# A bidirectional RWKV-7 layer on one core: readers of the side jobs' small products and the projections' evictions placed some dense blocks later, and their bank handed out in turn

## Chip, core and metric

The kernel runs on one core of a Trainium2 chip. The metric is the device time of one execution in microseconds; the number to forecast is the median over runs of the changed kernel. Before the change it is 3232.46 us (three runs, 3229.34 to 3234.77).

## What is computed

One layer over 128 context and 1024 latent tokens of width 1024: half a SwiGLU FFN, a token mixer, half a second FFN, each with a norm before and after and a modulation. The mixer is the part that the change touches. Cut to what matters:

```python
r, k, v, g, cb, cc, xc, gate_a, gate_b = split(h @ w_in)          # 5632 columns
kk = k*k_k;  kk = kk * rsqrt(sum(kk*kk over a head) + 1e-12)
for d in (0, 1):                                                   # forward, backward
    decay, a_d = small two-layer maps of h and its shifted copy
    k_d = k * (1 + (a_d - 1)*k_a)
    S = S*w_t + (S @ -kk_t) (kk_t*a_t)^T + v_t k_t^T ;  y_t = S @ r_t   # per head, per token
y = groupnorm(y_0 + y_1)*gn_gain + gn_bias + (bonus_0 + bonus_1)*v
y_a = (y*sigmoid(g)) @ w_branch_a
y_b = (cb * conv3(cc*xc)) @ w_branch_b
out = (sigmoid(gate_a)*y_a + sigmoid(gate_b)*y_b) @ w_out
```

## The kernel before

All tokens lie along the free axis in three tiles of 384; every dense product is float32 made of three fp32r matmuls (low weights by high input, high by low, high by high). Such a triple, 128 input rows deep, is called a *block* here. A projection column of `w_in` (128 outputs) takes 3 tiles by 8 blocks. The mixer has 1056 of them, numbered 1 to 1056 in the order in which TensorE runs them (L740 to L742, function `proj`).

The recurrence is done in chunks of 64 tokens, as 18 **items** (16 for the latent tokens, two heads' pairs `g` by eight steps `j`; 2 for the context). An item has three parts:

- `front` (function `stage_b`, once for each direction): loads of the operands, products `scr` (L1047) and `bkt` (L1062), masks, four copies `nn` (L1056);
- `solve`: the triangular systems, almost all of it on VectorE. It begins with one transpose `lm` (L1079), of which there is one for each item, goes through 15 pairs of a product `un` and a sum (L1088, L1089), a pair of transposes `xr` (L1108, L1109), and ends with small products `l64`, `l64b` on TensorE (L1116, L1127);
- `seq_latent` or `seq_ctx` (function `step`): two steps of the states in each direction (L1165 to L1199).

In step i the program writes front(i+1), the states of item i, solve(i+1). These three are called the **chain**, and get the highest priority with the scheduler, which puts the instructions of each engine into one fixed order. An engine runs its list in that order.

Beside the chain there are **side jobs**: `stage_k` (the normed kk and the bonus of one pair of heads and 256 tokens), `stage_v` (v turned into the state's layout), `finish` (group norm and gate of the result). Each is a generator that gives back, after each piece, a number of blocks to wait for. Three lanes (f, k, v) hold them. `fill(n)` takes n blocks from the projections (`filler`); after each it may advance one lane by one piece, and sets `PB.anchor` to that block. An instruction passed through `PB` is ordered behind the anchor on its engine's list. The small products of side jobs (`cps`, `kkb`, `bon`, `vt`, `gv`, `gm`, all at L177 by the wrapper) write to one PSUM bank, tag "oc", of which there is a single buffer. Their reader on VectorE or ScalarE follows in the program directly, with no anchor of its own (`rsq` at L238, L970, L978, L997, L1229).

The main loop has two ways of using up blocks: `fill(GI)` with GI = 40 after each item, and

```python
        def need(kind, g, *bs):
            while not all((kind, 2 * g + pp, b) in made for b in bs for pp in range(2)):
                fill(1)
```

before an item whose input a side job must have finished. Blocks used in `need` run beside side jobs only; the chain has nothing to do there once it has run dry. When `filler` is empty, `fill` goes on calling side jobs and gives TensorE nothing.

The projections' results are copied out of PSUM by ScalarE at `evict()`, called at the second block of the next tile (L750).

Of the kernel before, what the change touches and what calls it, by code (L numbers as in the profile page):

```python
# [13 lines left out]
AF = mybir.ActivationFunctionType  # L14
ALU = mybir.AluOpType
# [45 lines left out]
def body(ctx: ExitStack, tc: tile.TileContext, I: dict, y_prompt, y_sample, new_state):  # L61
# [120 lines left out]
    PB = Beside()  # L182
# [50 lines left out]
            V.scalar_tensor_tensor(out=y, in0=tt, scalar=1.5, in1=y, op0=ALU.add, op1=ALU.mult)  # L233
        return y

    def rsq(ps, n, scale, eps):
        x = tiny.tile([128, 16], F32, name="nx", tag="nx")[:, :n]
        V.tensor_scalar(out=x, in0=ps[:, :n], scalar1=scale, scalar2=eps, op0=ALU.mult, op1=ALU.add)  # L238
        return newton(x, n)

    def compact(sq, n, rhs, nr, scale, eps, tag="sc", PE=PE):
        ps = psp.tile([128, 16], F32, name="cps", tag=tag, bufs=1 if tag == "oc" else 2)
        for i in range(n):
            PE.matmul(ps[:, i * nr:(i + 1) * nr], sq[:, i * 128:(i + 1) * 128], rhs, start=True, stop=True)
        return rsq(ps, n * nr, scale, eps)

    def bcast(rs, sp, PE=PE):
        ps = psp.tile([128, TW], F32, name="bcps", tag="sc")
# [410 lines left out]
def mixer(nc, tc, pool, env):  # L659
# [68 lines left out]
    def proj(col, evac, ts=range(NT)):  # L728

        if col not in ahead:  # L730
            assert not plan or plan[0] == col
            if plan:
                fetch()
            else:
                ahead[col] = load_w(w_in[:, col:col + 128], 8, G)
        w = ahead.pop(col)
        for t in ts:
            ps = e.psp.tile([128, TW], F32, name="pj", tag="mm")
            for k, ((hi, lo), (xh, xl)) in enumerate(zip(w, hx(t))):
                PE.matmul(ps, lo, xh, start=(k == 0), stop=False)  # L740
                PE.matmul(ps, hi, xl, start=False, stop=False)  # L741
                ins = PE.matmul(ps, hi, xh, start=False, stop=(k == 7))  # L742
                clock["dense"] += 1
                if k == 0 and t == ts[0]:
                    fetch(ins)
                if k == 5 and t == ts[len(ts) > 1]:
                    for job in halves:
                        job()
                    halves.clear()
                if k == 1:  # L750
                    evict()
# [47 lines left out]
    with ExitStack() as ph:  # L799
# [15 lines left out]
            G.memset(t_, 0.0)  # L815
        HR = [slice(0, 64), slice(64, 128)]

        GI, GF, GL, GM, GC, SG_ = 40, 8, 16, 6, 14, 2
        def job_g(p):
            yield from proj(1536 + p * 128, to_dram(gd[p], AF.Tanh, scale=0.5))  # L820
            evict()
# [117 lines left out]
            return out  # L939


        def stage_k(p, t0, n, bon=True):

            while ("rkv", p) not in made:
                yield 1
            nt = n // 128
            k = q1.tile([128, 256], F32, name="ok", tag="ok")[:, :n]
            turned(k, mirrored(p, 5, -1, t0, n), PB.first)
            r = oload(opd[p][:, 3], t0, n, "or")
            f0, f1 = (q1.tile([128, 256], F32, name=f"o{x}", tag=f"o{x}")[:, :n] for x in "di")  # L950
            turned(f0, mirrored(p, 2, -1, t0, n))
            turned(f1, mirrored(p, 7, -1, t0, n))
            yield GL
            a = q1.tile([128, 256], F32, name="oa", tag="oa")[:, :n]
            PB.first(S.activation(out=a, in_=k, func=AF.Square, scale=e.KK_[:, p:p + 1]))
            b = f0
            PB.first(V.tensor_tensor(out=b, in0=f0, in1=f1, op=ALU.add))
            V.tensor_tensor(out=b, in0=b, in1=k, op=ALU.mult)
            V.scalar_tensor_tensor(out=b, in0=r, scalar=rk4[:, p:p + 1], in1=b, op0=ALU.mult, op1=ALU.mult)
            v = r  # L960
            SP.dma_start(v, vd[p][:, t0:t0 + n])
            yield 3
            rs = compact(a, nt, sel, 2, 1.0, 1e-12, "oc", PB)
            yield GC
            ps = ps_.tile([128, 256], F32, name="kkb", tag="oc", bufs=1)[:, :n]
            for i in range(nt):
                for h in range(2):
                    PB.matmul(ps[HR[h], i * 128:(i + 1) * 128], rs[:, 2 * i + h:2 * i + h + 1].to_broadcast([128, 64]), ident, start=True, stop=True)
            kk = a
            V.scalar_tensor_tensor(out=kk, in0=k, scalar=e.KK_[:, p:p + 1], in1=ps, op0=ALU.mult, op1=ALU.mult)  # L970
            for h, dst in enumerate(mirrored(p, 4, 1, t0, n)):
                SP.dma_start(dst, kk[HR[h]])
            made.add(("kk", p, (t0 - NCTX) // 256))
            yield 4
            ps = ps_.tile([128, 256], F32, name="bon", tag="oc", bufs=1)[:, :n]
            PB.matmul(ps, bones, b, start=True, stop=True)
            o = v
            V.tensor_tensor(out=o, in0=v, in1=ps, op=ALU.mult)  # L978
            S.activation(out=o, in_=o, func=AF.Identity, bias=gb4[:, p:p + 1])
            SP.dma_start(bvd[p][:, t0:t0 + n], o)  # L980
            yield GF

        def stage_v(p, t0, n, zv):
# [4 lines left out]
                yield 1  # L988
            v = oload(vd[p], t0, n, "lv", PB.first)
            yield GL  # L990
            ps = ps_.tile([128, 4, 64], F32, name="vt", tag="oc", bufs=1)
            for i in range(nb):
                for h in range(2):
                    hr, kr = HR[h], HR[1 - h]
                    PB.matmul(ps[kr, i], v[hr, i * 64:i * 64 + 64], cent[hr] if t0 >= NCTX else ident[hr, hr], start=True, stop=True)
            for h in range(2):
                S.activation(out=zv[HR[1 - h], 0:nb, p % 2, HR[h]], in_=ps[HR[1 - h], 0:nb], func=AF.Copy)  # L997
            made.add(("vt", p, (t0 - NCTX) // 256))

        def turned(dst, srcs, first=lambda ins: None):  # L1000
# [206 lines left out]
        def finish(p, t0, n, y):  # L1207
# [5 lines left out]
            yc = q1.tile([128, 256], F32, name="yc_", tag="f3")[:, :n]  # L1213
            yo = y
            if t0 < NCTX:
                ps = ps_.tile([128, 256], F32, name="gm", tag="oc", bufs=1)[:, :n]
                PB.matmul(ps, bones, y, start=True, stop=True)
                V.scalar_tensor_tensor(out=yc, in0=ps, scalar=-1.0 / 64, in1=y, op0=ALU.mult, op1=ALU.add)
                yo = yc
            a = q1.tile([128, 256], F32, name="ysq", tag="f4")[:, :n]  # L1220
            PB.first(S.activation(out=a, in_=yo, func=AF.Square))
            yield GM
            rs = compact(a, nt, sel, 2, 1.0 / 64, 64e-5, "oc", PB)
            yield GC
            ps = ps_.tile([128, 256], F32, name="gv", tag="oc", bufs=1)[:, :n]
            for i in range(nt):
                for h in range(2):
                    PB.matmul(ps[HR[h], i * 128:(i + 1) * 128], rs[:, 2 * i + h:2 * i + h + 1].to_broadcast([128, 64]), ident, start=True, stop=True)
            V.tensor_tensor(out=yc, in0=yo, in1=ps, op=ALU.mult)  # L1229
# [293 lines left out]
```

## Time and profile before

| | us |
|---|---|
| median of three runs | 3232.46 |
| lowest, highest | 3229.34, 3234.77 |
| the profiled execution's own time | 3226.22 |
| its span, first to last instruction | 3224.3 |

Busy shares over the span: TensorE 93%, VectorE 57%, ScalarE 36%, GpSimd 14%. They are means over stages that are limited by different things. The scan with its side jobs and projections takes the stretch from about 1060 to 2131 us; ahead of it lie the first FFN and the two-layer maps, behind it the two branches, the output projection and the second FFN.

To read it: of a stretch of the span, the windows view gives the busy time of each engine with the number of its instructions in parentheses, then the granted TensorE clock (1.00 is full speed), the share of the DMA engines and the bytes moved. Since the chain begins anew with each `lm`, the time between two `lm` is the length of an item.

### The profile page before, as it was taken

Reading aid. Unit: us, or ns where it says so; the run is one execution under the profiler, and the core shown is the slowest. Engines: PE = TensorE matmul, PEld = TensorE weight load, DVE = VectorE, ACT = ScalarE, POOL = GpSimd, SP = SyncE. Lnnn points to the kernel's source line nnn. Section 1 sums busy time; section 2 is a strip of 40 time slices with the busy share of each in tenths; the row PEclk is TensorE's granted clock in tenths of the full one; section 3 lists DMA queues with packets and bytes.
Section 4 is the critical chain, followed back from the end, with each engine's and each line's share of the span. In section 5 each row is a group of like instructions: output and inputs, shape, how many; then the busy total and the mean of one; then the engine's idle time right before and its main releaser. Section 6 shows DMA issues by size and latency. Waiting matters only on the chain.

```text
span 3224.3 us, 55042 instructions
## 1 busy us (share of the span) xinstructions
PE 3005.2 (93%) x21284; PEld 2836.3 (88%) x21284; DVE 1821.8 (57%) x4148; ACT 1151.7 (36%) x2618; POOL 453.8 (14%) x436
## 2 busy tenths in 40 slices
PE   8999999999989989988898898679989999999998
PEld 5999999999979987877777777469989999999998
DVE  7535655654875344566875668665782323323356
ACT  5421121113545424354544445332543111121244
POOL 1000000000241121333322322100220000000012
PEclk9999999999989999999999999779989999999999
DMA  8422333324534542322333223236432111111244
GB/s 271 148 63 85 111 89 92 99 79 126 163 118 133 178 132 66 111 81 79 90 114 105 88 86 108 62 112 190 141 99 66 46 38 49 46 38 45 84 144 131
DMA packets 483898, 330.80 MB, mean 103 GB/s; under 512 B 49768, under 2 KB 461748, under 8 KB 483636
## 3 DMA queue, kind: packets, MB, share of 16 engines
q1 hardware_dynamic: 483008, 326.80, 33.9%
q8 instruction: 167, 2.74, 0.4%
q14 instruction: 95, 0.78, 0.1%
q10 hardware_dynamic: 308, 0.44, 0.0%
q0 software_dynamic: 320, 0.04, 0.0%
HBM read 265.58 MB, written 61.60 MB: 101 GB/s over the span
## 4 chain that ended last, share of the span: by engine, by line
PE 69%; DVE 17%; ACT 5%; issue 4%; DMA 3%; POOL 1%; SPq 0%; DVEq 0%; ACTq 0%; POOLq 0%
PE po L220 6%; PE po L219 6%; PE po L221 6%; PE pg L220 5%; PE pg L219 5%; PE pg L221 5%; PE pu L220 5%; PE pu L219 5%; PE pu L221 5%; PE pj L742 3%; PE pj L740 3%; PE pj L741 3%; DVE un L1088 2%; PE scr L1047 2%; DMA ops<-opd 1%
## 5 line engine op out<-in xcount | busy, mean ns | idle before, releaser
L138 ACT ACTIVATE whi<-wst 128x512 fp32r<-128x512 f32 (+1 forms) x578 | 350.4, 611 | 731.6 <-PE po L221 393.1
L139 DVE TENSOR_TENSOR wlo<-wst,whi 128x512 fp32r<-128x512 f32 (+1 forms) x480 | 326.7, 681 | 305.4 <-ACT whi L138 296.1
L740 PE MATMUL pj<-hh,wlo 128*128 128x384 f32 x1056 | 375.4, 355 | 0.3 <-ACT fso L768 0.3
L741 PE MATMUL pj<-hl,whi 128*128 128x384 f32 x1056 | 371.1, 351 | 2.7 <-POOL hl L269 1.4
L742 PE MATMUL pj<-hh,whi 128*128 128x384 f32 x1056 | 371.3, 352 | 0.0
L220 PE MATMUL pg<-hl,whi 128*128 128x384 f32 x1056 | 356.8, 338 | 5.3 <-POOL hl L269 2.9
L219 PE MATMUL po<-ah,wlo 128*128 128x384 f32 x1056 | 357.1, 339 | 3.8 <-ACT ah L138 3.8
L219 PE MATMUL pg<-hh,wlo 128*128 128x384 f32 x1056 | 357.7, 339 | 1.9 <-DVE wlo L139 1.3
L220 PE MATMUL po<-al,whi 128*128 128x384 f32 x1056 | 356.3, 338 | 0.4 <-DVE al L139 0.4
L221 PE MATMUL pg<-hh,whi 128*128 128x384 f32 x1056 | 356.1, 337 | 0.0
L221 PE MATMUL po<-ah,whi 128*128 128x384 f32 x1056 | 355.7, 337 | 0.0
L219 PE MATMUL pu<-hh,wlo 128*128 128x384 f32 x1056 | 355.4, 337 | 0.0
L220 PE MATMUL pu<-hl,whi 128*128 128x384 f32 x1056 | 354.0, 335 | 0.0
L221 PE MATMUL pu<-hh,whi 128*128 128x384 f32 x1056 | 354.0, 335 | 0.0
L279 POOL TENSOR_TENSOR ss<-ss,sqt 128x384 f32<-128x384 f32 x78 | 88.7, 1140 | 1695.8 <-ACT sqt L278 1691.3
L432 DVE TENSOR_TENSOR sil<-sil,pu 128x384 f32<-128x384 f32 x132 | 72.8, 552 | 352.7 <-PE pu L221 352.6
L404 DVE TENSOR_TENSOR o<-o,po 128x384 f32<-128x384 f32 x288 | 159.0, 552 | 172.4 <-PE po L221 171.4
L741 PEld LDWEIGHTS pj<-hl,whi 128*128 128x128 f32 x1056 | 204.3, 193 | 9.9 <-issue 3.0
L740 PEld LDWEIGHTS pj<-hh,wlo 128*128 128x128 f32 x1056 | 203.7, 193 | 10.4 <-issue 5.7
L742 PEld LDWEIGHTS pj<-hh,whi 128*128 128x128 f32 x1056 | 204.2, 193 | 7.4 <-issue 3.3
L220 PEld LDWEIGHTS pg<-hl,whi 128*128 128x128 f32 x1056 | 200.1, 189 | 7.8 <-DVE hl L271 3.9
L219 PEld LDWEIGHTS po<-ah,wlo 128*128 128x128 f32 x1056 | 198.6, 188 | 4.8 <-ACT ah L138 4.8
(584 smaller groups left out, 5746.9 us busy)
## 6 DMA issues: line engine op xcount, KB each, us to landing
wst<-in_ffn_w SPq DMA_DIRECT2D x324, 256.0 KB, 2.9
wmod<-in_w_mod SPq DMA_DIRECT2D x144, 256.0 KB, 2.8
wst<-in_w_in SPq DMA_DIRECT2D x94, 256.0 KB, 3.3
ops<-opd SPq DMA_DIRECT2D x36, 640.0 KB, 4.5
wst<-in_ffn_w SPq DMA_DIRECT2D x96, 192.0 KB, 2.5
xo<-xd SPq DMA_DIRECT2D x64, 192.0 KB, 3.9
wst<-in_w_out SPq DMA_DIRECT2D x48, 256.0 KB, 2.8
opd<-zv SPq DMA_DIRECT2D x24, 384.0 KB, 2.8
```

Of the source, the lines that this page charges most:

```text
L138: first(S.activation(out=hi, in_=src, func=AF.Copy))
L139: eng.tensor_tensor(out=lo, in0=src, in1=hi.bitcast(F32), op=ALU.subtract)
L219: PE.matmul(ps, lo, xh, start=(k == 0), stop=False)
L220: PE.matmul(ps, hi, xl, start=False, stop=False)
L221: later.tick(PE.matmul(ps, hi, xh, start=False, stop=(k == nk - 1)))
L279: eng.tensor_tensor(out=ssum, in0=ssum, in1=q, op=ALU.add)
L404: V.tensor_tensor(out=O[m][t], in0=O[m][t], in1=ps, op=ALU.add)
L432: V.tensor_tensor(out=s, in0=s, in1=pu, op=ALU.mult)
L740: PE.matmul(ps, lo, xh, start=(k == 0), stop=False)
L741: PE.matmul(ps, hi, xl, start=False, stop=False)
L742: ins = PE.matmul(ps, hi, xh, start=False, stop=(k == 7))
L1047: PE.matmul(ps[64 * o:64 * o + 64, i], BK[64 * h:64 * h + 64, o, i * 64:i * 64 + 64], E[64 * h:64 * h + 64, s0 + i, h], start=True, stop=True)
```

## The change

1. `evict()` is called at the fourth block of the next tile and not at the second.
2. The reader of each small product is given back to the lane for GV = 4 blocks more, and is then ordered behind the block that is current (`PB.first`).
3. A lock: a job that wants the bank calls `take()`, which waits in steps of 7 blocks while another job holds it; after the reader the lock is cleared.

Arithmetic, operands and transfers stay the same.

```diff
-    def rsq(ps, n, scale, eps):
+    def rsq(ps, n, scale, eps, first=lambda ins: None):
...
-        V.tensor_scalar(out=x, in0=ps[:, :n], scalar1=scale, scalar2=eps, op0=ALU.mult, op1=ALU.add)
+        first(V.tensor_scalar(out=x, in0=ps[:, :n], scalar1=scale, scalar2=eps, op0=ALU.mult, op1=ALU.add))
...
-                if k == 1:
+                if k == 3:
                     evict()
...
-        GI, GF, GL, GM, GC, SG_ = 40, 8, 16, 6, 14, 2
+        GI, GF, GL, GM, GC, SG_, GV = 40, 8, 16, 6, 14, 2, 4
...
+        held = []
+
+        def take():
+
+            while held:
+                yield 7
+            held.append(1)
...
-            rs = compact(a, nt, sel, 2, 1.0, 1e-12, "oc", PB)
+            yield from take()
+            ps = e.sums(a, nt, sel, 2, "oc", PB)
+            yield GV
+            rs = e.rsq(ps, 2 * nt, 1.0, 1e-12, PB.first)
+            held.clear()
             yield GC
+            yield from take()
             ps = ps_.tile([128, 256], F32, name="kkb", tag="oc", bufs=1)[:, :n]
...
-            V.scalar_tensor_tensor(out=kk, in0=k, scalar=e.KK_[:, p:p + 1], in1=ps, op0=ALU.mult, op1=ALU.mult)
+            yield GV
+            PB.first(V.scalar_tensor_tensor(out=kk, in0=k, scalar=e.KK_[:, p:p + 1], in1=ps, op0=ALU.mult, op1=ALU.mult))
+            held.clear()
```

The same three lines (`take`, `yield GV`, `PB.first` with the lock cleared) go round `bon`, `vt`, both products of `finish`, and, without the wait, `gm`.

Both kernels have the same 1056 blocks, but they stand elsewhere against the chain. Line numbers of the changed kernel are 3 higher in `proj` and 24 higher from `stage_b` on.

**First place: TensorE, where item 2 begins.** `pj` is a block's matmul, `hhT_t` its input (row group, then tile of tokens), `scr` the first product of the item's `front`, `sq` and `yp` those of the states. Before:

```order
L740 MATMUL pj_12694<-hh7_0_8311,wlo_12569 128x384
L741 MATMUL pj_12694<-hl7_0_8312,whi_12568 128x384
L742 MATMUL pj_12694<-hh7_0_8311,whi_12568 128x384
L740 MATMUL pj_12745<-hh0_1_8826,wlo_12565 128x384
L741 MATMUL pj_12745<-hl0_1_8827,whi_12564 128x384
L742 MATMUL pj_12745<-hh0_1_8826,whi_12564 128x384
L1047 MATMUL scr_12922<-e0_12905,ops_12907 64x128
```

Now:

```order
L743 MATMUL pj_13156<-hh1_2_9343,wlo_12962 128x384
L744 MATMUL pj_13156<-hl1_2_9344,whi_12961 128x384
L745 MATMUL pj_13156<-hh1_2_9343,whi_12961 128x384
L743 MATMUL pj_13156<-hh2_2_9352,wlo_12962 128x384
L1071 MATMUL scr_13401<-e0_13384,ops_13386 64x128
```

The first `scr` of item 2 stood behind block 393; it stands behind block 498 now, four projection columns later.

**Second place: TensorE, where the blocks end.** `l64` is the product that ends a solve, `cps`, `gv`, `kkb` and `bon` are products of side jobs. Before:

```order
L740 MATMUL pj_21574<-hh7_2_9402,wlo_21047 128x384
L741 MATMUL pj_21574<-hl7_2_9403,whi_21046 128x384
L742 MATMUL pj_21574<-hh7_2_9402,whi_21046 128x384
L1186 MATMUL yp_21364<-ab0_20604,zv2_9436 64x64 x4
L1186 MATMUL yp_21364<-ab1_20605,zv1_9435 64x64 x4
L1177 MATMUL yp_21770<-e0_21187,zv0_9434 64x64 x4
L1177 MATMUL yp_21770<-e1_21188,zv0_9434 64x64 x4
L177 MATMUL cps_21522<-cst_81,ysq_21499 128x2 x2
```

Now:

```order
L743 MATMUL pj_18865<-hh7_2_9401,wlo_18658 128x384
L744 MATMUL pj_18865<-hl7_2_9402,whi_18657 128x384
L745 MATMUL pj_18865<-hh7_2_9401,whi_18657 128x384
L1071 MATMUL scr_18946<-e1_18878,ops_18931 64x128
L1071 MATMUL scr_18947<-e1_18878,ops_18931 64x128
```

The last block stood in the middle of item 16; it now stands ahead of the second `front` of item 10.

**Third place: TensorE, the end of the solve of item 11.** Before:

```order
L742 MATMUL pj_18733<-hh1_0_8144,whi_18295 128x384
L740 MATMUL pj_18733<-hh2_0_8173,wlo_18296 128x384
L741 MATMUL pj_18733<-hl2_0_8174,whi_18295 128x384
L1127 MATMUL l64b_18167<-xr_18138,x8_18104 32x32
L1165 MATMUL sq_18471<-zv3_9437,e1_17859 64x64 x4
L1165 MATMUL sq_18471<-zv0_9434,e0_17858 64x64 x4
L1127 MATMUL l64b_18168<-xr_18138,x8_18104 32x32
L1047 MATMUL scr_18380<-e0_18363,ops_18365 64x128 x8
```

Now:

```order
L1140 MATMUL l64_19525<-xr_19522,ab0_19237 32x32 x2
L1140 MATMUL l64_19525<-xr_19522,ab1_19238 32x32 x2
L1151 MATMUL l64b_19551<-xr_19522,x8_19488 32x32
L1189 MATMUL sq_19722<-zv3_9437,e1_19243 64x64 x4
L1189 MATMUL sq_19722<-zv0_9434,e0_19242 64x64 x4
L1151 MATMUL l64b_19552<-xr_19522,x8_19488 32x32
L1071 MATMUL scr_19631<-e0_19614,ops_19616 64x128 x8
```

The chain's products keep their own sequence; the blocks between them are gone, here and in every item from 11 on. Counted over the whole list, the blocks ahead of the first products of the two directions' fronts are:

| front of item | 0 | 1 | 2 | 9 | 10 | last block |
|---|---|---|---|---|---|---|
| before, 1st / 2nd direction | 214 / 259 | 295 / 296 | 393 / 438 | 717 / 718 | 758 / 809 | in item 16 |
| now | 260 / 316 | 353 / 354 | 498 / 554 | 829 / 831 | 1006 / 1056 | in item 10 |

## Rows read from the trace of the kernel before

**Rows 1.** The page: busy times by engine; TensorE's granted clock in 40 slices.

```profile
PE 3005.2 (93%) x21284; PEld 2836.3 (88%) x21284; DVE 1821.8 (57%) x4148; ACT 1151.7 (36%) x2618; POOL 453.8 (14%) x436
...
PEclk9999999999989999999999999779989999999999
```

**Rows 2.** Windows view of the mixer's stretches: PE, PEld, DVE, ACT, POOL, PEclk, DMA, GB/s.

```profile
1351.00:1664.00 313.00, 272.58 (x2987) 233.72 (x2986) 229.74 (x667) 143.38 (x394) 107.29 (x105) 0.95 0.32 92
1664.00:1724.00 60.00, 56.68 (x745) 44.80 (x736) 41.44 (x135) 32.71 (x98) 14.31 (x15) 1.00 0.31 91
1767.00:2030.00 263.00, 234.47 (x2666) 200.22 (x2662) 181.75 (x543) 128.52 (x368) 77.72 (x79) 0.96 0.33 97
2030.00:2069.00 39.00, 22.23 (x326) 18.45 (x328) 30.17 (x102) 14.57 (x40) 7.50 (x9) 0.78 0.25 76
2069.00:2131.00 62.00, 31.81 (x392) 24.11 (x392) 39.66 (x165) 14.46 (x50) 1.15 (x4) 0.56 0.09 24
```

**Rows 3.** Source view of the transpose that begins each solve; then VectorE's timeline at two.

```profile
L1079 DVE STREAM_TRANSPOSE lm<-nn x18: 1231/1239/1246, 1190.7 to 2069.3; 128x1024 f32<-128x1024 f32 x18
...
1767.49 1.25 DVE L1079 STREAM_TRANSPOSE lm<-nn 128x1024 f32<-128x1024 f32 x1
...
2030.23 1.24 DVE L1079 STREAM_TRANSPOSE lm<-nn 128x1024 f32<-128x1024 f32 x1
```

**Rows 4.** Timeline of TensorE at 2030 us: third matmul of consecutive blocks (start, us).

```profile
2030.91 0.33 PE L742 MATMUL pj<-hh,whi 128*128 128x384 f32 x1
...
2031.95 0.34 PE L742 MATMUL pj<-hh,whi 128*128 128x384 f32 x1
```

**Rows 5.** Windows view of 20 us inside a wait for side jobs.

```profile
1280.00:1300.00 20.00, 20.00 (x121) 19.52 (x120) 8.92 (x21) 5.37 (x11) 6.11 (x6) 1.00 0.17 47
```

**Rows 6.** Groups by line on VectorE, 1351 to 1664 us: busy us, mean ns, idle before.

```profile
L848 DVE SCALAR_TENSOR_TENSOR cnv<-ccs,cw,cnv 128x378 f32<-128x378 f32 (+2 forms) x12 | 9.2, 770 | 0.0
L232 DVE TENSOR_TENSOR nt<-nt,nx 128x4 f32<-128x4 f32 x36 | 8.3, 231 | 0.1
L233 DVE SCALAR_TENSOR_TENSOR ny<-nt,ny 128x4 f32<-128x4 f32 x36 | 7.4, 205 | 0.1
L847 DVE SCALAR_TENSOR_TENSOR cnv<-ccs,cw,cnv 128x378 f32<-128x378 f32 (+2 forms) x12 | 6.9, 575 | 2.0 <-ACT cnv L842 1.9
L231 DVE SCALAR_TENSOR_TENSOR nt<-ny 128x4 f32<-128x4 f32 x36 | 6.3, 174 | 0.1
L957 DVE TENSOR_TENSOR od<-od,oi 128x256 f32<-128x256 f32 x6 | 4.9, 822 | 0.0
L978 DVE TENSOR_TENSOR or<-or,bon 128x256 f32<-128x256 f32 x5 | 2.0, 402 | 2.8 <-PE bon L177 2.8
L238 DVE TENSOR_SCALAR nx<-cps 128x4 f32<-128x4 f32 x12 | 1.9, 154 | 3.2 <-PE cps L177 3.1
```

**Rows 7.** Waits, 1135 to 2140 us: total, times, longest.

```profile
ACT fso L768 <- PE pj L742: 77.7, 34, 4.5
DVE nx L238 <- PE cps L177: 41.0, 17, 8.3
DVE oa L970 <- PE kkb L177: 25.4, 7, 5.9
DVE or L978 <- PE bon L177: 17.3, 9, 2.9
```

**Rows 8.** Timeline: one form on VectorE beside GpSimd's weight split and without it.

```profile
1492.26 1.51 DVE L1040 TENSOR_TENSOR e<-ops,fl 64x256 f32<-64x256 f32 x1
...
1490.79 2.71 POOL L139 TENSOR_TENSOR wlo<-wst,whi 128x512 fp32r<-128x512 f32 x2 [2.79 <-ACT whi L138]
...
2036.55 0.41 DVE L1040 TENSOR_TENSOR e<-ops,fl 64x256 f32<-64x256 f32 x1
```

**Rows 9.** Timeline of TensorE: 16 products of a front at either clock.

```profile
1424.97 1.09 PE L1047 MATMUL scr<-e,ops 64*64 64x128 f32 x16
...
2057.73 1.97 PE L1047 MATMUL scr<-e,ops 64*64 64x128 f32 x16
```

More of the change, by code (lines that the diff above doesn't have):

```diff
@@ L234, in newton, with sums @@
         return y
-    def rsq(ps, n, scale, eps):
+    def rsq(ps, n, scale, eps, first=lambda ins: None):
         x = tiny.tile([128, 16], F32, name="nx", tag="nx")[:, :n]
-        V.tensor_scalar(out=x, in0=ps[:, :n], scalar1=scale, scalar2=eps, op0=ALU.mult, op1=ALU.add)
+        first(V.tensor_scalar(out=x, in0=ps[:, :n], scalar1=scale, scalar2=eps, op0=ALU.mult, op1=ALU.add))
         return newton(x, n)
-    def compact(sq, n, rhs, nr, scale, eps, tag="sc", PE=PE):
+    def sums(sq, n, rhs, nr, tag="sc", PE=PE):
         ps = psp.tile([128, 16], F32, name="cps", tag=tag, bufs=1 if tag == "oc" else 2)
@@ L244, in compact @@
             PE.matmul(ps[:, i * nr:(i + 1) * nr], sq[:, i * 128:(i + 1) * 128], rhs, start=True, stop=True)
-        return rsq(ps, n * nr, scale, eps)
+        return ps
+    def compact(sq, n, rhs, nr, scale, eps, tag="sc", PE=PE):
+        return rsq(sums(sq, n, rhs, nr, tag, PE), n * nr, scale, eps)
     def bcast(rs, sp, PE=PE):
@@ L974, in stage_k @@
             yield 4
+            yield from take()
             ps = ps_.tile([128, 256], F32, name="bon", tag="oc", bufs=1)[:, :n]
@@ L977, in stage_k @@
             o = v
-            V.tensor_tensor(out=o, in0=v, in1=ps, op=ALU.mult)
+            yield GV
+            PB.first(V.tensor_tensor(out=o, in0=v, in1=ps, op=ALU.mult))
+            held.clear()
             S.activation(out=o, in_=o, func=AF.Identity, bias=gb4[:, p:p + 1])
@@ L990, in stage_v @@
             yield GL
+            yield from take()
             ps = ps_.tile([128, 4, 64], F32, name="vt", tag="oc", bufs=1)
@@ L995, in stage_v @@
                     PB.matmul(ps[kr, i], v[hr, i * 64:i * 64 + 64], cent[hr] if t0 >= NCTX else ident[hr, hr], start=True, stop=True)
+            yield GV
             for h in range(2):
-                S.activation(out=zv[HR[1 - h], 0:nb, p % 2, HR[h]], in_=ps[HR[1 - h], 0:nb], func=AF.Copy)
+                PB.first(S.activation(out=zv[HR[1 - h], 0:nb, p % 2, HR[h]], in_=ps[HR[1 - h], 0:nb], func=AF.Copy))
+            held.clear()
             made.add(("vt", p, (t0 - NCTX) // 256))
@@ L1215, in finish @@
             if t0 < NCTX:
+                yield from take()
                 ps = ps_.tile([128, 256], F32, name="gm", tag="oc", bufs=1)[:, :n]
@@ L1219, in finish @@
                 yo = yc
+                held.clear()
             a = q1.tile([128, 256], F32, name="ysq", tag="f4")[:, :n]
@@ L1222, in finish @@
             yield GM
-            rs = compact(a, nt, sel, 2, 1.0 / 64, 64e-5, "oc", PB)
+            yield from take()
+            ps = e.sums(a, nt, sel, 2, "oc", PB)
+            yield GV
+            rs = e.rsq(ps, 2 * nt, 1.0 / 64, 64e-5, PB.first)
+            held.clear()
             yield GC
+            yield from take()
             ps = ps_.tile([128, 256], F32, name="gv", tag="oc", bufs=1)[:, :n]
@@ L1228, in finish @@
                     PB.matmul(ps[HR[h], i * 128:(i + 1) * 128], rs[:, 2 * i + h:2 * i + h + 1].to_broadcast([128, 64]), ident, start=True, stop=True)
-            V.tensor_tensor(out=yc, in0=yo, in1=ps, op=ALU.mult)
+            yield GV
+            PB.first(V.tensor_tensor(out=yc, in0=yo, in1=ps, op=ALU.mult))
+            held.clear()
             V.scalar_tensor_tensor(out=yc, in0=yc, scalar=gg4[:, p:p + 1], in1=bv, op0=ALU.mult, op1=ALU.add)
```

## Prediction

> **What bounds the kernel now.** I read the page first. TensorE is busy 93% of the span [rows 1], so at first sight only its work counts. The page's clock line falls in two places, and the second of them, ahead of the second FFN, is the end of the scan [rows 1]. So the next view is that of the windows over the scan. There TensorE is busy 272.58 of 313 us while items 2 to 8 run, and only 22.23 of 39 us in the item in which the blocks run out [rows 2]. VectorE is busy 229.74 of the same 313 us.
>
> Then the items themselves. There are 18 transposes that open a solve, the last at 2069.3 us; item 10's is at 1767.49, item 16's at 2030.23 [rows 3]. So six items with blocks among them take 262.7 us, 43.8 each. The seventh, which has only the last 7 blocks in its first microseconds, takes 39.0. This comparison decides the case. An item loses some 38 blocks and gets 5 us shorter, though a block alone takes TensorE 0.52 us (two of them from 2030.91 to 2031.95) [rows 4], and 38 take 20 us. An item is therefore not as long as TensorE's work but as long as the chain, which lies mostly on VectorE: 30.17 us busy in the item without blocks, 181.75/6 = 30.3 in those with them [rows 2]. The blocks fill TensorE's waiting time. A block put beside the chain is nearly free; one that runs where the chain stands still costs its whole 0.52 us. In such a stretch TensorE is full: 121 matmuls in 20.00 busy us of 20 [rows 5].
>
> **The change part by part.** It adds no matmul, no operation and no transfer; the lock is the generator's, and no engine sees it. What it moves is the place of the blocks, and this the order of the changed kernel shows exactly.
>
> *Blocks put ahead of the chain, first part.* Three lanes now wait in turn for one bank, in steps of 7 blocks, and each of their products holds it for 4 blocks more. The items' `need` goes on drawing blocks until the jobs are through. The second front of item 2 comes 554 blocks in, before it was 438. The side jobs ahead of it are the same, so the 116 blocks are bare: 116 x 0.52 = **+60 us**.
>
> *Items 2 to 8.* From that front to the first of item 9 there are 275 blocks for 279: **-2 us**.
>
> *Second part.* From item 9's first front to item 10's there were 41 blocks and are 177. 136 x 0.52 = 71 us. The old stretch took 60 us with 3.3 us of TensorE idle [rows 2]; I set that against the products of the side jobs that are run there now instead of in items 2 to 8. **+71 us**.
>
> *What items 2 to 8 lose.* Some side jobs and projections no longer meet the chain there, since they run in the two stretches above. Of the three convolutions' 216 blocks 118 remain, so 45% of 9.2 + 6.9 us on VectorE go: -7. Of 12 root computations 8 remain; their 23.9 us (1.9 + 6.3 + 8.3 + 7.4) are 2.0 each: -8. Two `stage_k` and three `finish` fewer have 19 other operations, at 402 ns as the bonus reader: -8. The waits for `cps` and `bon`, which later readers are spared, are 3.2 + 2.8: -6. All from [rows 6]; together -29 us. VectorE is busy 73% of that stretch, and what leaves in its idle time gains nothing. I take two thirds, **-20 us**, between 0 and -29.
>
> *The tail.* All 245 blocks that followed item 10's second front are gone from there; the last block now ends just ahead of it. Items 10 to 16 run bare. They took 262.7 + 39.0 = 301.7 us. If nothing but TensorE's blocks set their length they would lose 245 x 0.52 = 127 us; if the chain alone did, nothing. The nearest row is the item that is nearly bare, 39.0 us, which held 7 blocks and the usual side jobs. Two things favour a little less than that. GpSimd's weight splits end with the blocks, and beside one of them VectorE's product of 0.41 us took 1.51 [rows 8]. And the jobs of `stage_k` leave the later items. One thing speaks for more: the clock, below. I take 38.5 us for each of the seven, 269.5 in all: **-32 us**, between 0 and -127.
>
> *The end of the blocks.* The store of the last kk and the load behind it have about six blocks less above them when item 10's second front waits for it: **+2 us**, between 0 and +6. From 2069 to 2131 us no block ran before either [rows 2]: no change in these 62 us.
>
> *The evictions and readers.* ScalarE waited 77.7 us in 34 pieces for a projection's last matmul [rows 7]. Two blocks later is 1.04 us later, so about half of each wait could go. ScalarE is 36% busy over the span [rows 1] and works beside VectorE's solve; where these waits fell in an item, VectorE was working. I cost the edit at 0; if that cover were missing, up to -35 us would be had. The PSUM buffer that it frees later is one of two, and is wanted only when the next tile begins, four blocks on.
>
> Sum: 60 - 2 + 71 - 20 - 32 + 2 = **+79 us**, against the profiled execution's 3226.2 us: 3305. The median of the runs shown lies 6.2 us above that execution, so the forecast for the median is **3311 us**.
>
> **A rule against it.** In the bare item the granted clock was 0.78, and 0.56 in the 62 us after it [rows 2]; sixteen products of a front took 1.97 us there, 1.09 among blocks [rows 9]. The engine stood idle for 17 of 39 us before and while the clock was low. So bare items pay at the lower of the two levels, 1.2 and not 2.4 GHz, for products that the chain waits for. The row of 39.0 us has this in it already, for most of one item. The Trainium skill, "TensorE: Matmul & The Clock Gate", section "HAM oscillation — how this bites in real kernels", says that bursts parted by long waits put the array back to half its clock each time. By that rule alone seven bare items in a row would lose more than one did, which is the third rival below; the trace agrees with the rule's direction, and only the size is open.
>
> **The rivals.** *Faster.* TensorE is the limit in an item after all, and a bare item is shorter by its 20 us of blocks. Then the tail loses 127 us, items 2 to 8 all of their 29: 60 - 2 + 71 - 29 - 127 + 2 = -25, 3207 us. For it speaks TensorE's 234.47 of 263 us in the items with blocks. It decides from the point where the tail saves the other terms' 111 us, at (301.7 - 111)/7 = 27.2 us an item. VectorE alone is busy 30.17 us in the bare item [rows 2], and it took 39.0.
>
> *No change.* The readers' waits for `cps`, `kkb` and `bon` lay on the chain. They are 41.0 + 25.4 + 17.3 = 83.7 us [rows 7], of which I counted 6. All of them gone would give +79 - 78 = +1, 3233 us. Against it: while items 2 to 8 ran, the waits for `cps` and `bon` were 6.0 us [rows 6], so the long ones lie in the stretches where TensorE is full and the chain stands still.
>
> *Cold tail.* Bare items run at the low clock throughout and are as long as filled ones, 7 x 43.8 = 306.6, 5 more than before. Then 60 - 2 + 71 - 20 + 5 + 2 = +116, 3348 us.
>
> *Short tail.* Side jobs fall into the gaps of the fronts, and a bare item needs 33 us, 3 more than VectorE's busy time. The tail gives 71: +40, 3272 us.
>
> That the change doesn't do what it says, because a bank with one buffer is taken in turn anyway, would leave the blocks where they were. The order shows that it doesn't.
>
> **Chances.** Forecast 0.71, cold tail 0.13, short tail 0.08, no change 0.04, faster 0.04. A measurement of this kernel can tell about 0.2%, 6 us, from no change. All cases but the last two are slower by more: slower 0.92, same 0.04, faster 0.04. The likeliest case has its own range from its unknowns (relief 0 to -29, tail -10 to -50): 3285 to 3345. The range that takes in most of both tails is 3265 to 3350; outside are the faster case, no change, and half of the cold tail.
>
> **What would show it.** In the changed kernel's profile: the opening transposes of items 0 to 2 come later, the third by about 60 us; item 10's by about 110; no `pj` after it; seven items of 37 to 40 us each with TensorE's clock near 0.6 to 0.8 and its busy share near half; items 3 to 8 a few us shorter each; waits of VectorE for `cps`, `kkb` and `bon` nearly gone, with no gain to be seen for it. I am wrong if bare items are under 30 us, if the chain in the long stretches is not at rest, or if the stages outside 1060 to 2131 us change.

## The result, and the profile after

The changed kernel takes 3366.8 us (median of four runs, 3363.97 to 3369.65) against 3233.6 us for the kernel before in the same comparison: ratio 1.0413 [1.0398, 1.0429], 133 us slower. The forecast was 3311 us with a range that ended at 3350; its direction held, its size did not. The profiled executions differ by 141.3 us of span, 3224.3 and 3365.6.

The page of the changed kernel: busy times, then TensorE's busy share and granted clock in 40 slices.

```profile
PE 3028.2 (90%) x21284; PEld 2870.4 (85%) x21284; DVE 1823.9 (54%) x4148; ACT 1149.0 (34%) x2618; POOL 456.4 (14%) x436
...
PE   8999999999889989888999645549989999999998
...
PEclk9999999999989989989999765559999999999999
```

The same instructions ran, and VectorE, ScalarE and GpSimd worked as long as before [rows 1]. The clock's fall ahead of the second FFN, two slices at 7 before, is five slices now, down to 5. The windows of the changed kernel, cut at the transposes that open a solve (columns as in [rows 2]):

```profile
1254.00:1407.00 153.00, 142.68 (x1184) 130.00 (x1182) 65.91 (x172) 56.89 (x150) 45.61 (x40) 0.97 0.30 87
1407.00:1721.00 314.00, 274.85 (x3029) 235.42 (x3029) 225.04 (x613) 145.86 (x405) 108.79 (x106) 0.93 0.31 90
1721.00:1898.00 177.00, 163.15 (x1376) 147.89 (x1375) 74.54 (x240) 61.76 (x163) 31.02 (x27) 0.95 0.37 113
1898.00:2193.00 295.00, 147.39 (x2218) 120.48 (x2218) 187.45 (x603) 114.27 (x347) 59.60 (x69) 0.60 0.17 48
2154.00:2193.00 39.00, 18.66 (x284) 15.64 (x284) 24.27 (x78) 11.63 (x33) 7.37 (x9) 0.61 0.01 3
2193.00:2273.00 80.00, 36.61 (x407) 27.97 (x407) 47.86 (x188) 14.89 (x53) 1.23 (x5) 0.53 0.12 34
```

They are item 1 with the wait for item 2, items 2 to 8, the stretch from item 9 to item 10, the seven bare items, the last of them by itself, and the end. Their bounds are these transposes (source view, then VectorE's timeline):

```profile
L1103 DVE STREAM_TRANSPOSE lm<-nn x18: 1230/1237/1247, 1214.7 to 2192.7; 128x1024 f32<-128x1024 f32 x18
...
1407.22 1.25 DVE L1103 STREAM_TRANSPOSE lm<-nn 128x1024 f32<-128x1024 f32 x1
...
1897.94 1.25 DVE L1103 STREAM_TRANSPOSE lm<-nn 128x1024 f32<-128x1024 f32 x1
```

Against the same transposes before [rows 3], where the time came from:

| stretch | before, us | after, us | change | forecast |
|---|---|---|---|---|
| start to item 2 | 1349.4 | 1407.2 | +57.8 | +60 |
| items 2 to 8 | 325.8 | 313.4 | -12.4 | -2 - 20 |
| item 9 to item 10 | 92.2 | 177.3 | +85.0 | +71 + 2 |
| items 10 to 16 | 301.8 | 294.8 | -7.0 | -32 |
| last transpose to the first branch product | 62.0 | 80.7 | +18.7 | 0 |
| behind it | 1093.0 | 1092.2 | -0.8 | 0 |
| sum | | | +141.3 | +79 |

Three questions follow. Is it the place of the blocks that costs the time, or the later readers and evictions themselves? Why do seven items without blocks take as long as items with them? What lengthened the end?

### The profile page after: what moved, and what is told of

Same layout as the page of the kernel before. It is cut to its first block, busy times and chain, and to the rows that moved or that the text cites. A ratio compares the mean times of both kernels' runs of the same rounds, so it can differ in the third digit from the quotient of the medians.

```text
span 3365.6 us, 55093 instructions
## 1 busy us (share of the span) xinstructions
PE 3028.2 (90%) x21284; PEld 2870.4 (85%) x21284; DVE 1823.9 (54%) x4148; ACT 1149.0 (34%) x2618; POOL 456.4 (14%) x436
## 4 chain that ended last, share of the span: by engine, by line
PE 72%; DVE 17%; ACT 4%; DMA 3%; issue 3%; POOL 1%; SPq 0%; DVEq 0%; ACTq 0%; POOLq 0%
PE po L220 6%; PE po L219 6%; PE po L221 6%; PE pg L220 5%; PE pg L219 5%; PE pg L221 5%; PE pu L219 5%; PE pu L220 5%; PE pu L221 5%; PE pj L743 4%; PE pj L744 4%; PE pj L745 4%; DVE un L1112 3%; PE scr L1071 2%; DMA ops<-opd 1%
```

## The experiments

In the expectations, A is the account of the forecast: what a block costs is set by whether the chain runs beside it. Each run's profile is read at the same transposes. The table gives the start of the first solve, of items 2, 9, 10 and 17, the first branch product, the span (us), and the median of the timed runs.

```
kernel               0       2       9      10      17     branch   span    median
before            1190.7  1349.4  1675.2  1767.5  2069.3  2131.3  3224.3
changed           1214.7  1407.2  1720.7  1897.9  2192.7  2273.4  3365.6  3366.8
116 blocks early  1251.0  1413.0  1728.4  1817.3  2126.9  2188.6  3280.6  3284.1
lock, no pause    1189.6  1346.1  1677.2  1769.5  2074.7  2136.9  3228.0  3233.9
evictions alone   1188.0  1345.7  1676.2  1764.2  2071.9  2133.9  3223.9  3224.9
spare blocks      1214.9  1403.7  1717.4  1893.4  2171.2  2253.1  3344.9  3345.9
hand-over         1210.6  1392.3  1706.3  1868.5  2167.3  2243.1  3333.4  3334.8
tail unpaused     1216.1  1404.7  1719.3  1899.0  2191.8  2252.5  3341.5  3340.6
spare + unpaused  1212.4  1404.4  1715.0  1890.5  2170.2  2237.4  3322.5  3327.1
changed, short    1186.0  1333.6  1648.1  1774.5  2082.0  2150.4  3242.7  3243.7
short + evictions 1165.1  1290.9  1620.1  1673.8  1970.5  2071.6  3153.5  3158.1
short             1166.3  1289.7  1615.1  1668.0  1970.9  2070.4  3153.2  3159.6
shorter           1161.6  1285.2  1620.7  1665.5  1977.1  2086.0  3168.0  3169.2
```

**What a block costs where the chain waits.** The kernel before, with 116 blocks taken ahead of the first side jobs. Readers, bank and evictions stay as they were.

```diff
+        fill(116)
         side(ks(0, 0, 3) + vs(0, 0, 3))
         need("kk", 0, 0, 3)
```

> The kernel before, with one edit: 116 blocks of the projections are run ahead of the first side jobs, where the chain has not begun (the number that the change puts ahead of item 2). No reader, no eviction, no lock is moved. Theory A (the time lies in blocks that run where the chain stands still): +60 us from 116 x 0.52; the blocks end 116 earlier, in item 14, so two to three items are bare and each gets about 3 us shorter: together +50 to +60 us, some 3287 us. Theory B (the time lies in the later readers, evictions and the lock themselves, since they hold up the side jobs): 0, within 6 us of the kernel before. Theory C (TensorE sets the length of an item): the bare items give back 20 us each, so the sum is 0 to +10.

Measured: 3284.1 us, ratio 1.016 [1.0134, 1.0185], 52 us slower. The first solve comes 60.3 us later (116 x 0.52), and nearly all of that is still there at the last one. The blocks end in item 13 now, so that items 14 to 16 run bare; they take 48.4, 43.8 and 41.0 us against 48.1, 44.1 and 39.0 before. So 116 blocks in the wrong place are a price of 52 us with none of the change's other parts, and three bare items give none of it back. The end behind them takes 61.7 us, as before the change (62.0).

**The later readers without their pauses.** The changed kernel without its `yield GV` lines and with the evictions at their old place. The lock and the readers' anchors stay.

```diff
-            yield GV
             rs = e.rsq(ps, 2 * nt, 1.0, 1e-12, PB.first)
...
-                if k == 3:
+                if k == 1:
```

> The changed kernel without the pause of 4 blocks between product and reader and with the evictions back at the second block; what is left is that the readers are ordered behind the block that is current, and a lock that is never contended. The blocks stand against the chain as in the kernel before. Theory A: within 6 us of the kernel before. Theory B: slower by more than 10 us.

Measured: 3233.9 us (10 runs), ratio 1.0006 [0.9994, 1.0018]. With no pause between a product and its reader the lock is never found held, and nothing is left of the 133 us. The loss therefore comes in through the pauses and the lock that they keep held, not through anchoring the readers. A pause without the lock was not run.

**The evictions alone.** The kernel before with `k == 3` in `proj`.

```diff
-                if k == 1:
+                if k == 3:
```

> The kernel before, with the evictions at the fourth block and nothing else. Theory A: within 6 us of the kernel before, since ScalarE's waits for a projection (77.7 us in 34 pieces) are covered by VectorE's work in the items and by TensorE's in the long stretches; about half of these waits go. Theory B: if these waits lay on the chain, 10 to 35 us faster; if the later release of the PSUM buffer holds up the next tile, slower by more than 6.

Measured: 3224.9 us (10 runs), ratio 0.9972 [0.996, 0.9983]: 7 us faster. Its profiled execution does not show where; its branch begins 2.6 us later than before and its span is 0.4 us shorter. The part of the change that I priced at 0 is a small gain.

**Is the tail held by the clock?** After the last product of each front the changed kernel gets 40 blocks that recompute a projection already done and whose result nobody reads, once the real blocks are used up: 22244 matmuls for 21284, 320 more blocks. Of these 233 run in items 10 to 16 and 87 behind the last transpose. The cut shows the call alone, not the function.

```diff
+            spare_blocks(n)
             for _ in range(n):
                 PB.anchor = next(filler, PB.anchor)
```

> The changed kernel, with 40 spare blocks given to TensorE in each item after the projections have run out, so that items 10 to 16 are filled again. The spare blocks multiply the last projection's weights by the first token tile into a PSUM buffer that nobody reads; the outputs stay the same. Chain alone (a block beside the chain costs nothing): items 10 to 16 take 294.6 us in the changed kernel and stay within 10 us of that. Cold clock (bare items are long because TensorE runs at its lower level): with the clock back near 0.95 these items get 2 to 4 us shorter each, 15 to 30 us in all. Blocks get in the way: each item 2 to 3 us longer, up to the 43.8 us that filled items took before, +15 to +20 us. TensorE's bound: +20 us an item, +140 us.

Measured: 3345.9 us, ratio to the kernel before 1.0352 [1.0335, 1.0369], 21 us faster than the changed kernel although TensorE has 320 blocks more to do. Its page:

```profile
PE 3157.8 (94%) x22244; PEld 2988.4 (89%) x22244; DVE 1825.5 (55%) x4148; ACT 1148.5 (34%) x2618; POOL 461.0 (14%) x436
...
PEclk9999999999989999989999799999999999999999
```

Items 10 to 16 take 277.8 us in place of 294.8, at this granted clock (windows of the whole tail, of its last item, and of the end):

```profile
1893.00:2171.00 278.00, 245.48 (x2921) 207.79 (x2919) 187.85 (x605) 113.66 (x346) 59.37 (x69) 0.93 0.18 50
...
2136.60:2171.00 34.40, 32.23 (x390) 28.10 (x390) 23.91 (x77) 11.04 (x32) 6.87 (x9) 1.00 0.02 6
...
2171.00:2253.00 82.00, 71.25 (x671) 62.26 (x669) 49.67 (x191) 17.04 (x57) 1.77 (x5) 0.93 0.14 41
```

VectorE works as long as in the changed kernel, 187.85 for 187.45 us. What became shorter is the chain's own products. Groups by line on TensorE over items 11 to 15 (busy us, mean ns | idle before), first of the changed kernel,

```profile
L1071 PE MATMUL scr<-e,ops 64*64 64x128 f32 x320 | 26.4, 345 | 0.6 <-ACT e L1075 0.6
L1189 PE MATMUL sq<-zv,e 128*64 128x64 f32 x160 | 11.1, 319 | 11.0 <-DVE zv L1218 11.0
L1140 PE MATMUL l<-xr,ab 32*32 32x32 f32 x160 | 4.8, 240 | 39.2 <-DVE xr L1132 31.0 <-DVE ny L233 6.6 <-DVE nt L232 1.1
```

then with the spare blocks:

```profile
L1072 PE MATMUL scr<-e,ops 64*64 64x128 f32 x320 | 18.8, 277 | 2.4 <-ACT e L1076 2.2
L1190 PE MATMUL sq<-zv,e 128*64 128x64 f32 x160 | 7.7, 246 | 3.2 <-DVE zv L1219 3.2
L1141 PE MATMUL l<-xr,ab 32*32 32x32 f32 x160 | 3.5, 195 | 1.6 <-DVE xr L1133 1.5
```

The three groups went from 42.3 to 30.0 busy us. The first product after a solve, `l`, no longer follows an idle TensorE (39.2 us to 1.6). The tail as a whole is 17 us shorter. The gain is not even: items 10 to 12 take 36.6, 41.6 and 41.2 us for 36.8, 41.6 and 40.6, and it lies in items 13 to 16, 3.2 to 6.1 us each. Item 11 shows why it can be nothing. VectorE's waits in it (total, times, longest), first of the changed kernel, then with the spare blocks:

```profile
DVE ab L1072 <- PE scr L1071: 9.9, 2, 5.2
...
DVE e L1063 <- PE sq L1189: 0.4, 1, 0.4
...
DVE ab L1073 <- PE scr L1072: 7.4, 2, 4.0
...
DVE e L1064 <- PE sq L1190: 2.8, 1, 2.8
```

The wait for `scr` is 2.5 us shorter at the higher clock, and a later one, for `sq`, 2.4 us longer with blocks in TensorE's list. In this item TensorE (its blocks left out) and VectorE run the same list in both kernels; in items 13 to 15 both lists have side jobs at other places. So the 17 us are what clock, blocks and the new order make together: that the clock is the larger part is likely, but its share by itself is not shown. The other 4 us of the median's 21 stand ahead of the tail, where there is no spare block.

**How much of it is the lock's step of seven blocks?** A job that finds the bank held now gives its lane's turn to another and looks again at the next call.

```diff
-                yield 7
+                yield None
...
+                    if gap is None:
+                        return False
```

> The changed kernel, with one edit to the lock: a job that waits for the bank takes it as soon as it is free, and its waiting doesn't use up a turn of the lanes (in the changed kernel each look after 7 blocks takes such a turn). The 4 blocks between product and reader stay. The second front of item 2 then stands behind 537 blocks (before 441, changed 557), that of item 10 behind 1028 (811, 1056). Theory A (blocks where the chain stands still, 0.52 us each): the two stretches have 20 and 8 blocks fewer, -10 to -15 us against the changed kernel, and up to 10 more at the end of the scan, if fewer side jobs are left over there: 3342 to 3357 us. Theory D (the looks of the waiting jobs are what costs): most of the 133 us come back, below 3280 us.

Measured: 3334.8 us, ratio 1.0324 [1.0297, 1.0351], 32 us faster than the changed kernel. The blocks ahead of the second fronts of items 0, 2 and 10 are 307, 534 and 1027, against 316, 554 and 1056 with the step and 259, 438 and 809 before. The step causes part of the loss, and 7 us more of it than I had allowed at most. Most stays; that this is the bank being still held for four blocks by every product is argued, not shown. The variant in which the step is one block was not tried.

**What lengthened the end?** The changed kernel, but once all 1056 blocks are used a side job's pauses are 0, save the lock's own.

```diff
-                        self.at = clock["now"] + gap
+                        self.at = clock["now"] + (0 if clock["dense"] >= 1056 and gap != 7 else gap)
```

> The changed kernel, but once the projections have run out a side job's pauses are nought, so that its pieces are handed on at every turn (a waiting job still looks every 7). The end of the scan, from the opening transpose of item 17 to the first product of the branches, takes 80.7 us in the changed kernel and 62.0 in the kernel before. Theory L (side jobs left over, because each takes more turns): the end falls back to 60 to 66 us; items 10 to 16 may get up to 8 us longer together; 3350 to 3360 us in all. Theory K (the end is longer because TensorE is cold there): the end stays at 80 us; with the spare blocks of the run before, which filled half of it, it had stayed at 81.9.

Measured: 3340.6 us, ratio 1.0343 [1.0315, 1.037], 26 us faster. The end, 80.7 us in the changed kernel, takes 60.7; its window:

```profile
2192.00:2253.00 61.00, 31.49 (x383) 23.69 (x378) 38.53 (x165) 14.83 (x51) 1.22 (x4) 0.56 0.09 25
```

VectorE has 165 instructions there, as many as before the change [rows 2] and 23 fewer than the changed kernel. The 23 are roots and products of `finish`, of side jobs that had not come through by the last item and ran one after another behind it. The clock is as low as ever in this end, so the clock is not what made it longer. With the spare blocks the end has a clock of 0.93 and still takes 81.9 us, though their 87 blocks in it may hide a gain. The whole gain, 26 us, is 9 more than I had expected at best.

**Both of these together**, the spare blocks and the tail without pauses:

> The changed kernel with both repairs of its tail: 40 spare blocks in each bare item (result unread, outputs the same) and no pauses of the side jobs once the projections have run out. If the cold clock and the side jobs left over are separate terms, their gains add: 21 us (3367 to 3346) and 26 us (3367 to 3341) give 3320 us, within 8. If they are one and the same time, it is 3335 to 3346 us. What is left above the kernel before is then the two long stretches, 143 us later than before at item 10 less what items 2 to 8 gave, some 85 to 95 us.

Measured: 3327.1 us, ratio 1.0302 [1.0279, 1.0325], 40 us faster than the changed kernel, where the two alone gave 21 and 26. The tail from item 10's transpose to the branch is 346.8 us, 17 less than before the change (363.8). What is left above the kernel before, 98 us of span, has its place ahead of item 10, whose transpose is 123 us late.

**The pauses the other way.** If pauses draw blocks where the chain waits, shorter ones than before must win. First the changed kernel with four of the old pauses cut by a third to a half and its own GV and lock kept:

```diff
-        GI, GF, GL, GM, GC, SG_, GV = 40, 8, 16, 6, 14, 2, 4
+        GI, GF, GL, GM, GC, SG_, GV = 40, 4, 10, 4, 8, 2, 4
```

> The changed kernel with the same shorter pauses, its lock and the 4 blocks between product and reader kept. Its second fronts stand behind 268 blocks (item 0), 439 (item 2), 868 (item 10); in the kernel before behind 261, 441, 811. Theory A (only the blocks' place against the chain counts): nearly the kernel before: about -1 us up to item 2, 63 more blocks between items 9 and 10, +33 us, one more bare item at no gain, up to 10 for side jobs left at the end, -7 for the evictions: 3255 to 3280 us. Theory B (lock and readers cost by themselves): still 100 us or more above the kernel with short pauses and above 3290 us.

Measured: 3243.7 us, ratio 1.004 [1.0025, 1.0055], 123 us faster than the changed kernel. 265, 436 and 865 blocks stand ahead of the three second fronts now. The second number is about that of the kernel before (438); the third still exceeds its 809 by 56, and the stretch from item 9 to item 10 is 34 us longer than before. I had expected 3255 to 3280 us.

Then the kernel before with the same pauses, together with the later evictions:

```diff
-        GI, GF, GL, GM, GC, SG_ = 40, 8, 16, 6, 14, 2
+        GI, GF, GL, GM, GC, SG_ = 40, 4, 10, 4, 8, 2
```

> The other way round: the kernel before with shorter pauses of the side jobs (after the loads 10 blocks for 16, between root and its use 8 for 14, in finish 4 for 6, after the bonus 4 for 8), and the evictions at the fourth block. Nothing of the readers or of a lock. The second fronts then stand behind 216 blocks (item 0, before 261), 333 (item 2, 441), 656 (item 10, 811), and 131 blocks are left when the scan ends; they run at full rate behind it. Theory A: some 40 to 60 blocks more run beside the chain than before, and no item is bare: 20 to 30 us faster, and 7 from the evictions as measured; waits of TensorE for roots that are not ready may take back up to 15. 3200 to 3222 us. Theory B (the pauses keep the engines from waiting for each other, and what they save is larger): slower than the kernel before by 10 us or more.

Measured: **3158.1 us**, ratio 0.9787 [0.9758, 0.9815], 75 us faster than before and 209 faster than the changed kernel. Its page, TensorE's busy share and clock:

```profile
PE   8999999999998998888888989999899999999998
...
PEclk9999999999999999999999999999999999999999
```

Neither dip of the clock is left. Its windows: items 2 to 8, item 9 to 10, items 10 to 16, the end, the first of the branch, and item 16 by itself:

```profile
1291.00:1620.00 329.00, 285.36 (x3190) 244.40 (x3188) 245.98 (x720) 153.18 (x420) 113.92 (x112) 0.95 0.33 96
1620.00:1674.00 54.00, 50.86 (x587) 41.95 (x586) 37.16 (x107) 28.45 (x81) 14.96 (x15) 0.95 0.28 78
1674.00:1970.00 296.00, 267.39 (x3176) 227.77 (x3174) 216.67 (x675) 152.25 (x440) 94.19 (x95) 0.99 0.31 92
1970.00:2071.00 101.00, 92.98 (x742) 85.16 (x743) 56.57 (x191) 37.71 (x97) 12.90 (x14) 0.93 0.40 123
2071.00:2110.00 39.00, 39.00 (x227) 39.00 (x226) 22.40 (x42) 9.00 (x16) 0.00 (x0) 1.00 0.50 148
...
1931.10:1970.50 39.40, 36.36 (x449) 31.41 (x447) 33.12 (x116) 17.88 (x50) 11.46 (x13) 1.00 0.19 60
```

In the terms of the forecast: to item 2 -58.6 us, items 2 to 8 +3.5, item 9 to 10 -38.6, items 10 to 16 -5.1, the end +39.1, behind it -11.1; together -70.8 of span. I had expected 3200 to 3222 us, at most half of the gain. Part of what I missed is the end. 130 blocks stand there now, 68 us at 0.52, and they lengthen it by 39: TensorE was busy 31.81 of 62 us there, at a clock of 0.56 [rows 2], and the blocks run beside the last side jobs. The branch then begins with a full TensorE; whether this is the whole of the 11 us behind it was not taken apart.

The pauses alone, with the evictions at their old place:

> The kernel before with the shorter pauses of run e7_short_e alone, the evictions back at the second block. If the shorter pauses make the whole gain of that run (75 us), the time is that of e7_short_e within 6 us, some 3158 us; if the later evictions are worth the 7 us that they showed alone, it is 3163 to 3168 us; if the two only work together (an eviction that waits holds up more when the side jobs are closer), above 3175 us.

Measured: 3159.6 us, ratio 0.9775 [0.976, 0.9789]. The pauses make the whole gain; beside them the evictions' 7 us cannot be seen.

And shorter pauses still, with the later evictions (40, 2, 8, 3, 5, 2):

> As the run before, with still shorter pauses (8, 5, 3, 2). Theory A: another 20 blocks fewer where the chain stands still, up to 10 us faster than the run before; but 5 blocks are 2.6 us, about as long as VectorE needs for a root when nothing else stands in its list (10 operations of 0.2 us), so waits of TensorE eat some of it: -10 to +15 us against the run before. Theory B: slower again by 10 us or more.

Measured: 3169.2 us, ratio 0.9811 [0.9787, 0.9835]. Item 10 comes 8 us earlier yet, the branch 14 us later: 156 blocks are left for the end, whose length is 108.9 us. Of the three lengths tried the middle one is the best, by 11 us over this one, though single runs of the two overlap (3155 to 3170 and 3162 to 3171 us).

## Why the prediction was right in sign and wrong in size

*Blocks put ahead of the chain, first part* (+60): measured +57.8. Right, and the run with 116 early blocks shows the price by itself.

*Items 2 to 8* (-2 - 20): measured -12.4. The blocks and the side jobs left as the order had said, but what they took with them was over-sized: 23 us of VectorE's work and 6 of its waits. [rows 2] and [rows 6] stop at 1664 us, 11 us short of item 9's transpose. Over the whole of items 2 to 8 before the change the window is

```profile
1349.40:1675.30 325.90, 284.60 (x3157) 242.96 (x3154) 237.33 (x682) 152.92 (x419) 113.64 (x112) 0.95 0.31 90
```

and VectorE's busy time fell from 237.33 to 225.04 us, by 12.3, as much as the stretch got shorter. Its groups over these items after the change (busy us, mean ns | idle before):

```profile
L850 DVE SCALAR_TENSOR_TENSOR cnv<-ccs,cw,cnv 128x378 f32<-128x378 f32 (+2 forms) x8 | 5.9, 736 | 0.0
L233 DVE SCALAR_TENSOR_TENSOR ny<-nt,ny 128x4 f32<-128x4 f32 x24 | 7.7, 319 | 0.2
L232 DVE TENSOR_TENSOR nt<-nt,nx 128x4 f32<-128x4 f32 x24 | 6.9, 286 | 0.2
L231 DVE SCALAR_TENSOR_TENSOR nt<-ny 128x4 f32<-128x4 f32 x24 | 6.5, 272 | 0.2
L998 DVE TENSOR_TENSOR or<-or,bon 128x256 f32<-128x256 f32 x4 | 1.6, 412 | 0.0
L238 DVE TENSOR_SCALAR nx<-cps 128x4 f32<-128x4 f32 x8 | 1.2, 148 | 0.8 <-PE cps L177 0.8
```

The root computations fell from 12 to 8 as forecast, but their four lines still take 22.3 us (1.2 + 6.5 + 6.9 + 7.7) where they took 23.9 [rows 6]: the three forms with means of 174 to 231 ns have means of 272 to 319 ns now. I multiplied a count by an old mean, and the mean moved. The operations themselves did not become slower; a larger share of them overlaps GpSimd's. Of the three forms' 108 operations before, the 94 that overlap no instruction of GpSimd take 151 ns on average, and of 72 now, 54 take 153. The other 14 and 18 take 558 and 711. A slow one and the next fast one (timeline of VectorE and GpSimd after the change):

```profile
1498.62 1.26 POOL L1059 TENSOR_TENSOR ops<-ops 128x512 f32<-128x512 f32 x1
1498.78 2.09 DVE L233 SCALAR_TENSOR_TENSOR ny<-nt,ny 128x4 f32<-128x4 f32 x1
1499.85 1.00 POOL L843 TENSOR_TENSOR ccs<-ccs,xcs 128x384 f32<-128x384 f32 x1
1500.90 0.16 DVE L231 SCALAR_TENSOR_TENSOR nt<-ny 128x4 f32<-128x4 f32 x1
```

That is what [rows 8] shows of another operation. The readers' waits went as said: 3.2 to 0.8 us for `cps`, 2.8 to 0.0 for `bon`.

*Second part* (+71 + 2): measured +85.0. TensorE is busy 163.15 of the 177 us, so this is TensorE's time, as argued. Nearly half of what is missing is one wait, on TensorE's timeline behind the last block; VectorE's wait ahead of it is shown first:

```profile
1885.87 0.42 DVE L1063 TENSOR_TENSOR e<-ops,fl 64x256 f32<-64x256 f32 x1 [3.33 <-DMA ops<-opd]
...
1888.34 0.69 PE L1071 MATMUL scr<-e,ops 64*64 64x128 f32 x4 [7.45 <-DVE ops L1060]
```

It is the load of the last kk, and VectorE's first operations on it, with no block left above them: the term that I put at +2 with an upper bound of 6. The rest was not taken apart.

*The tail* (-32): measured -7.0, the largest miss, and the step that failed. The mechanism was the forecast's, an item as long as the chain; the nearest row misled. I took item 16's 39.0 us as the sample of a bare item and 38.5 for each of the seven. They took 36.8, 41.6, 40.6, 43.3, 47.6, 46.0 and 38.7. Item 16 is a context item with half the state updates. The line of the state updates in the kernel before, in item 15 and in item 16 (VectorE's groups: busy us, mean ns | idle before):

```profile
L1194 DVE SCALAR_TENSOR_TENSOR zv<-sq,ft,zv 64x64 f32<-64x64 f32 x16 | 3.8, 277 | 0.5 <-PE sq L1185 0.3
...
L1194 DVE SCALAR_TENSOR_TENSOR zv<-sq,ft,zv 64x64 f32<-64x64 f32 x8 | 1.9, 275 | 0.1
```

So it was short because its chain does less, not because it was bare: in the kernel with short pauses and later evictions it holds 34 blocks at a clock of 1.00 and takes 39.4 us. Items 10 and 16 together took 75.5 us, 1.5 less than forecast; items 11 to 15 took 219.1 for 192.5, more than the whole miss. And even in item 16 removing work bought nothing: VectorE has 24.27 us in it after the change against 30.17 before [rows 2], and it takes 38.7 against 39.0. The clock is 0.61 for 0.78. Over the tail VectorE's busy time fell from 211.92 [rows 2] to 187.45 us, and the time hardly: it gave up work and got waits in exchange, for products at the low clock among them. I held that the row of 39.0 us had the clock's price in it already. With the spare blocks, which raise the clock, 17 of the 25 us by which the tail was missed come back. The other 8 are not separated. The rival of the cold tail, to which I gave 0.13 and +116 us, came nearest, and the spare blocks make its cause likely. That its sum is near 133 is partly luck, since it lacks the end's 18.7 us and the second part's 12. The Trainium skill, "TensorE: Matmul & The Clock Gate", section "HAM oscillation — how this bites in real kernels", says that short bursts of products between long waits for a transfer each begin at half clock. The tail's 0.60, between the levels of 1.2 and 2.4 GHz and close to the lower, and the spare blocks' 0.93 agree with it, though the waits here are for VectorE and ScalarE.

*The end* (0): measured +18.7. I put it at nothing on the ground that no block ran there before either. True, and beside the point: the side jobs that were delayed by pauses and lock had to end somewhere. The run without pauses in the tail gives 20.0 us back, all of it.

*Evictions and readers* (0): right for the readers, a gain of 7 us for the evictions. One sign that I named failed: the waits did not go away. From 1190 us to the branch, before the change (the first three lines) and after it:

```profile
DVE nx L238 <- PE cps L177: 33.3, 15, 8.3
DVE oa L970 <- PE kkb L177: 14.5, 5, 5.2
DVE or L978 <- PE bon L177: 13.0, 7, 2.9
...
ACT fso L771 <- PE pj L745: 103.7, 33, 5.3
...
DVE oa L987 <- PE kkb L177: 42.7, 9, 8.0
DVE nx L238 <- PE cps L177: 41.8, 20, 8.5
...
DVE or L998 <- PE bon L177: 22.6, 7, 4.2
```

VectorE's three are 107.1 us, 12 of them ahead of the first solve, and were 60.8; the 83.7 of [rows 7] begin 55 us earlier. Of the 107.1 us 0.8 lie in items 2 to 8 and 81.6 in the stretches ahead of items 2 and 10 (43.5 and 38.1), where the chain rests and TensorE is busy over 90%. That they cost nothing there is argued from this place, not tested.

Together the misses are -2.2, +9.6, +12.0, +25.0, +18.7 and -0.8 us: 62 us of span, over half of them in the tail and the end.

## What to carry to other kernels

In this kernel filler work has a price that depends on its place: 0.5 us a block where the dependent chain stands still, and little beside it, where taking 245 blocks away gave 7 us. A pause counted in blocks is a request for blocks in the first kind of place. So a change that makes helpers wait longer should be priced by the blocks that the consumer then draws, and by the helpers left over at the end; and the same knob should be tried the other way. Here that gave 3158 us, better than both kernels. A sample row for a new state of the program must do the same work as what it stands for: count its operations first.

## What was not expected of the hardware

Useless matmuls made the kernel faster: 320 blocks that nobody reads, 233 of them in items 10 to 16, raised the granted clock of these items from 0.60 to 0.93, and the items became 17 us shorter together. The real blocks of the kernel before had kept it at 0.96 over items 10 to 15 unseen [rows 2]. Their 245 x 0.52 = 127 us of work left the tail with the change, and the tail got 7 us shorter.
